# A 256-token stack on one core: the hybrid layers' activations, compression and pooling put in another order

## Chip, core and metric

The kernel runs on one core of a Trainium2 chip. The metric is device time in microseconds (us), the median of several executions. Inside the core five engines run side by side, each with its own queue of instructions: TensorE (PE, matrix products), VectorE (DVE), ScalarE (ACT), GpSimd (POOL) and SyncE (SP, which issues the DMAs). SBUF is the on-chip memory that all use; PSUM is the small memory that PE writes its products to.

## What is computed

A block of two layers (differential attention with a context, neighbourhood attention, each with a convolutional feed-forward part), then two hybrid layers. Sequence 256, width 1024, float32. The change touches the end of the block and the hybrid layers:

```python
def hybrid_layer(x, norm_g, w_in, ...):
    h = rmsnorm_2(x, norm_g)
    proj = h @ w_in
    (nsa_q, nsa_kv, nsa_g, pool_in, conv_in, fox_qkv, fox_f, gate_in, merge_in) = jnp.split(proj, split_at, axis=-1)
    o_nsa = nsa_mixer(nsa_q, nsa_kv, nsa_g, cmp_pos, cmp_w1, cmp_b1, cmp_w2, cmp_b2)
    o_pool = pool_mixer(pool_in, pool_w, pool_scale)
    c_x, c_b, c_c = jnp.split(conv_in, 3, axis=-1)
    o_conv = conv_mixer(c_x, c_b, c_c, conv_w)
    o_fox = fox_mixer(f_q, f_k, f_v, fox_f, fox_f_bias)
    for i, o in enumerate((o_nsa, o_pool, o_conv, o_fox)):
        branch = (o * jax.nn.silu(gates[:, :, i])) @ w_branch[i]
        term = jax.nn.sigmoid(merge[:, :, i]) * branch
        acc = term if acc is None else acc + term
    return x + acc @ w_out

def nsa_compress(k, pos_emb, w1, b1, w2, b2):       # inside nsa_mixer, for keys and for values
    blocks = k[:, idx] + pos_emb
    flat = blocks.reshape(B, nc, NSA_CMP_LEN * hd)
    return jax.nn.silu(flat @ w1 + b1) @ w2 + b2
```

The block before ends with `x = rmsnorm(x, norm_out)`, and the hybrid layer begins with a second norm of that.

## The kernel before

Activations lie transposed: `xT` has the 1024 features as eight chunks of 128 partitions, with the 256 tokens along the free axis. A float32 product is made from three products of rounded halves: a number is split into hi and lo, and `mm3` issues hi by hi (L335), weight hi by activation lo (L338) and weight lo by activation hi (L339). A projection of 128 output features ("a chunk") is 8 k steps of 3 matmuls, 24 matmuls of 256 columns.

Weights come by DMA from SP's queue into `raw` (3 buffers). `split` makes their halves: ACT copies to `whi` (L311), then `wlo` is raw minus whi (L314), on DVE, or on POOL for every `pool_every`-th split. Of `whi` and `wlo` there are 4 buffers each. PSUM has the tiles `acc` (2 buffers), `S` (3) and `misc` (3).

The order of each engine's instructions is not written out: a scheduler simulates the program and puts on each engine's queue what it finds ready first. Where the code asks for program order (`keep_in_program_order`) it keeps that.

The first hybrid layer (H0) starts inside the last down projection of the block: eight chunks of 33 matmuls each. As each chunk's residual lands in `xT` (L638, on DVE), `first_res` squares it for one norm (`norm_add`, ACT L474, summed on POOL L476), multiplies it by `norm_out` (L1035, DVE), squares it again for the second norm, and `scale_z` makes the hybrid's activation: a scaling by `g2` on DVE (L1161, tile `nt`), a rounded copy on ACT (L364) and a subtraction on DVE (L365), into `hhi` for both halves in H0 and `hlo` in H1. The norm factor itself is applied behind the products, as the broadcast tile `nbc` (L525 on PE, L530 on ACT). H1 starts the same way inside H0's output projection.

`hybrid` then runs, in this order: chunk 0 (`kvT`, keys and values to compress), chunks 1 and 2 (`kA`, `kB`, with `rope2`), the compression, chunks 3 and 4 (`q`), the product with `wvs` (48 matmuls of 400 columns, L1058 to L1062), NSA's scores (L1261), softmax (`softmax4`; POOL scales by L1531, PE transposes by L1535), FoX from chunks 5 to 8, the convolution from chunks 9 to 14, the pooling from chunks 15 and 16, the gates and the merge. The compression copies `kvT` into `big` with a position term (four DVE instructions, L1464), multiplies in two halves by DMAed weights (L1478, 16 products each), sums (L1485), applies a SiLU (DVE L1488, ACT L1492, DVE L1493 and L1494, tile `cu`) and multiplies again (L1496, L1497). The pooling makes sums over windows by doubling shifts on POOL (L1370, L1371), scales (L1376, L1377) and multiplies by `pool_w` (PE, L1379). In H0 eight POOL instructions (L1406) multiply `xT` by the norm's factor before the output projection needs it.

Of the kernel before, what the change touches and what calls it, by code (L numbers as in the profile page):

```python
# [195 lines left out]
def _layout_second(a, i):  # L196
    t1, wvs, mg, wb, wo, w1, w2, pw = [], [], [], [], [], [], [], []
    for l in range(DEPTH):
# [6 lines left out]
        tw = np.concatenate([kc, vc, ks, kw, kw, ks, q, fq, fk, cv, po, ga], axis=1)  # L205
# [22 lines left out]
class K:  # L228
# [355 lines left out]
    def ffn(self, l, halves, h_hi, h_lo, sts, mid=None, pre=(), bc=None):  # L584
# [4 lines left out]
        with self.pool(f"ffn{l}") as fp:  # L589
# [58 lines left out]
            for s in range(2):  # L648
# [22 lines left out]
                for m in range(8):  # L671
                    ws = self.wload(i["down"][l, s, m], [768, 640])
# [480 lines left out]
    def new_z(self, l):  # L1153

        z = self.t(self.hpool, [P, KC, 512], ("hhi", "hlo")[l], F32R)
        self.z = z[:, :, 0:T], z[:, :, T:512]

    def scale_z(self, l, kc):
        z = self.t(self.nrm, [P, T], "nt", bufs=5)
        k = l * KC + kc  # L1160
        self.nc.vector.tensor_scalar(z, self.xT[:, kc, 0:T], self.V("g2")[:, k : k + 1], None, op0=ALU.mult)  # L1161
        self.hilo(self.z[0][:, kc, :], self.z[1][:, kc, :], z)

    def hybrid(self, l, st, ns_out):
# [11 lines left out]
        self.pool_every, self.nsplit = 2, 1  # L1176
# [16 lines left out]
        def chunk(c):  # L1193

# [8 lines left out]
            w = self.split(queue.pop(0), 1024)  # L1203
            ps = (self.acc if 3 <= c < 99 else self.acc5)((P, T))
            self.proj(ps, w, zhi, zlo, T)
            return ps

# [43 lines left out]
        for kind, ty in (("slc", 1), ("win", 2)):  # L1251
            pT[kind] = t(hp, [P, 2, 4, T], "pT", bufs=2)
            for b in range(2):
                nk = P * (b + 1)
                sp = []
                for j in range(2):
                    s_ = self.sb((P, 2, T))
# [437 lines left out]
```

## Time and profile before

| | before |
|---|---|
| runs, us | 1627.94, 1636.3, 1638.55 (median 1636.3) |
| profiled execution, us | 1635.94 |
| span of its trace, us | 1634.0 |
| mean granted PE clock | 0.987 of full |
| H0 begins, at about | 1109.5 us |
| H1 begins, between | 1369 and 1405 us |

The trace shows one execution. A timeline row gives the start, the length, the engine, line, operation, output and inputs, and in brackets the idle time before it and what ended it. A line of the waits table gives an engine's waiting line, what it waited for, the total, the count and the longest wait. Lines L1161 and later are those of the kernel before; in the changed kernel the same code stands some 20 to 30 lines further down.

### The profile page before, as it was taken

How to read it: one execution, taken by the hardware profiler on the slowest of the kernel's cores; microseconds unless marked ns; L12 is line 12 of the kernel's file. 1: busy time of each engine (PE TensorE's matmuls, PEld its weight loads, DVE VectorE, ACT ScalarE, POOL GpSimd, SP SyncE). 2: the span in 40 equal slices, each digit the busy share in tenths (PEclk: the TensorE clock that was granted, in tenths of full speed). 3: DMA queues.
4: the chain of work that ended last, by engine and by line, in shares of the span. 5: the costliest groups of instructions: out<-in, count | busy, mean ns of one | idle time of the engine just before them, and what ended most of it. 6: DMA issues, size and time to landing. Idle time of an engine off the chain costs nothing.

```text
span 1634.0 us, 26740 instructions
## 1 busy us (share of the span) xinstructions
PE 1568.7 (96%) x10390; PEld 1367.3 (84%) x10390; DVE 1114.2 (68%) x1937; ACT 770.5 (47%) x1386; POOL 556.1 (34%) x505
## 2 busy tenths in 40 slices
PE   8999999899999999999999898997999999999998
PEld 5777677798888888877777887997899998899998
DVE  4657677678999994443445897567567668657665
ACT  3535454454422443334555653653654444545443
POOL 1122331331100111242234654667464226453222
PEclk9999999999999999999999999999999999999999
DMA  8523233225567532242322465546325555324552
GB/s 309 201 78 130 106 153 117 96 99 194 174 225 258 195 135 78 86 143 113 117 78 88 181 212 180 186 154 226 124 90 198 191 197 218 130 91 168 193 190 96
DMA packets 49486, 252.98 MB, mean 155 GB/s; under 512 B 5073, under 2 KB 8145, under 8 KB 31569
## 3 DMA queue, kind: packets, MB, share of 16 engines
q1 hardware_dynamic: 49360, 251.28, 43.0%
q8 instruction: 82, 1.34, 0.3%
q14 instruction: 44, 0.35, 0.1%
HBM read 250.21 MB, written 1.05 MB: 154 GB/s over the span
## 4 chain that ended last, share of the span: by engine, by line
PE 80%; DVE 11%; POOL 3%; issue 3%; ACT 2%; DMA 1%; SPq 0%; DVEq 0%; POOLq 0%; ACTq 0%
PE acc L335 11%; PE acc L338 11%; PE acc L339 11%; PE S L338 9%; PE S L335 9%; PE S L339 8%; PE S L1084 3%; DVE wlo L314 2%; PE misc L1131 1%; PE misc L1024 1%; PE S L1058 1%; PE misc L383 1%; PE S L1061 1%; DVE junk L436 1%; PE S L1062 1%
## 5 line engine op out<-in xcount | busy, mean ns | idle before, releaser
L311 ACT ACTIVATE whi<-raw 128x1024 fp32r<-128x1024 f32 (+2 forms) x374 | 374.1, 1006 | 428.9 <-PE S L338 161.9
L314 DVE TENSOR_TENSOR wlo<-raw,whi 128x1024 fp32r<-128x1024 f32 (+2 forms) x292 | 359.7, 1233 | 171.2 <-ACT whi L311 170.5
L335 PE MATMUL acc<-hhi,whi 128*128 128x256 f32 (+1 forms) x824 | 271.9, 330 | 1.7 <-DVE u L618 1.4
L338 PE MATMUL acc<-hlo,whi 128*128 128x256 f32 (+1 forms) x824 | 270.4, 328 | 0.3 <-DVE hlo L545 0.3
L339 PE MATMUL acc<-hhi,wlo 128*128 128x256 f32 (+1 forms) x824 | 268.9, 327 | 1.4 <-DVE wlo L314 1.4
L314 POOL TENSOR_TENSOR wlo<-raw,whi 128x1024 fp32r<-128x1024 f32 (+2 forms) x82 | 194.6, 2375 | 215.8 <-ACT whi L311 215.7
L335 PE MATMUL S<-hhi,whi 128*128 128x256 f32 (+1 forms) x560 | 178.3, 319 | 5.3 <-ACT hhi L364 3.2
L339 PE MATMUL S<-hhi,wlo 128*128 128x256 f32 (+1 forms) x560 | 177.7, 318 | 2.8 <-DVE wlo L314 2.3
L338 PE MATMUL S<-hlo,whi 128*128 128x256 f32 (+1 forms) x560 | 178.7, 319 | 0.1
L335 PEld LDWEIGHTS acc<-hhi,whi 128*128 128x128 f32 x824 | 155.5, 189 | 25.0 <-issue 10.0
L338 PEld LDWEIGHTS acc<-hlo,whi 128*128 128x128 f32 x824 | 154.8, 188 | 17.3 <-issue 5.3
L339 PEld LDWEIGHTS acc<-hhi,wlo 128*128 128x128 f32 x824 | 155.4, 189 | 15.8 <-DVE wlo L314 1.6
L624 POOL TENSOR_TENSOR u<-u,u 128x256 f32<-128x256 f32 (+1 forms) x46 | 59.2, 1288 | 273.8 <-ACT u L623 261.5
L436 DVE SCALAR_TENSOR_TENSOR junk<-araw,cb 128x1024 bf16<-128x1024 f32 x112 | 148.8, 1329 | 4.6 <-ACT cb L424 4.3
L335 PEld LDWEIGHTS S<-hhi,whi 128*128 128x128 f32 x560 | 105.1, 188 | 14.4 <-ACT hhi L364 3.4
L339 PEld LDWEIGHTS S<-hhi,wlo 128*128 128x128 f32 x560 | 105.0, 188 | 11.7 <-DVE wlo L314 2.9
L338 PEld LDWEIGHTS S<-hlo,whi 128*128 128x128 f32 x560 | 105.2, 188 | 7.4 <-DVE hlo L365 0.3
L1433 POOL TENSOR_TENSOR macc<-macc,mm 128x256 f32<-128x256 f32 x48 | 50.1, 1043 | 168.0 <-DVE mm L1431 168.0
L338 PE MATMUL acc<-hhi,whi 128*128 128x256 f32 x288 | 82.2, 286 | 0.0
L339 PE MATMUL acc<-hlo,wlo 128*128 128x256 f32 x288 | 81.7, 284 | 0.0
L335 PE MATMUL acc<-hlo,whi 128*128 128x256 f32 x288 | 81.4, 283 | 0.0
L335 PE MATMUL S<-ghi,whi 128*128 128x256 f32 (+1 forms) x231 | 76.3, 333 | 4.9 <-DVE xT L638 4.8
(414 smaller groups left out, 3777.7 us busy)
## 6 DMA issues: line engine op xcount, KB each, us to landing
raw<-in_up SPq DMA_DIRECT2D x44, 1024.0 KB, 4.8
raw<-in_mg SPq DMA_DIRECT2D x32, 1024.0 KB, 5.1
araw<-in_adav SPq DMA_DIRECT2D x56, 512.0 KB, 4.3
raw<-in_t SPq DMA_DIRECT2D x24, 1024.0 KB, 4.8
raw<-in_down SPq DMA_DIRECT2D x32, 704.0 KB, 4.1
raw<-in_ada SPq DMA_DIRECT2D x16, 1024.0 KB, 4.9
raw<-in_aqk SPq DMA_DIRECT2D x8, 1024.0 KB, 5.6
raw<-in_bqk SPq DMA_DIRECT2D x8, 1024.0 KB, 4.8
```

Of the source, the lines that this page charges most:

```text
L311: nc.scalar.activation(hi[:, :n], raw, AF.Copy)
L314: eng.tensor_tensor(lo[:, :n], raw, hi[:, :n].bitcast(F32), op=ALU.subtract)
L335: first = nc.tensor.matmul(ps, wh, x[0], start=start, stop=False)
L338: nc.tensor.matmul(ps, wh, x[1], start=False, stop=False)
L339: nc.tensor.matmul(ps, wl, x[0], start=False, stop=stop)
L383: nc.tensor.matmul(ps[32 * j : 32 * j + 32, 0:256], self.cs[:, 4 * r + j, :], raw[:, 4 * r + j, :], start=(r == 0), stop=(r == 1), tile_po ...
L436: nc.vector.scalar_tensor_tensor(junk, self.araw, 1.0, self.acb[0][:, c, :], op0=ALU.mult, op1=ALU.mult, accum_out=self.ada[l][:, v, k, c ...
L624: nc.gpsimd.tensor_tensor(us[0], us[0], us[1], op=ALU.mult)
L1024: nc.tensor.matmul(o[64 * j : 64 * j + 64, :], v[:, t, (2 * h + j) * 64 : (2 * h + j) * 64 + 64], pT[:, j, t, :], start=(t == 0), stop=(t ...
L1058: first = nc.tensor.matmul(ps, x[0], w[0], start=start, stop=False)
L1084: self.nc.tensor.matmul(sps[j][:, :n], q[a][r, qs], k[b][r, ks], start=(e == 0), stop=(e == 2))
L1433: nc.gpsimd.tensor_tensor(acc, acc, m, op=ALU.add)
```

## The change

Seven edits:

1. `scale_z` drops the scaled tile `nt`: ACT scales while it rounds, and DVE makes lo from `xT`, the gain and hi in one instruction.
2. The multiplication by `norm_out` leaves `first_res`: `g2` is multiplied by it once, the second norm squares with a gain, and POOL multiplies `xT` itself later, before the factor it already applied there.
3. `pool_every` is 0 from the sixth chunk of the last down projection on and through the hybrids' start; it is 2 again from FoX's chunks to the gates.
4. `chunks_late`: chunks 0 to 2 first run k steps 0 to 5, then steps 6 and 7 of each.
5. The compression is cut in two, `compress_in` behind the `q` chunks and `compress_out` behind `vs`.
6. The score loops go over the chunk first and the half second.
7. The pooling's chunks come before the convolution's (the weights are laid out in that order), its last product after the convolution.

```diff
-        tw = np.concatenate([kc, vc, ks, kw, kw, ks, q, fq, fk, cv, po, ga], axis=1)
+        tw = np.concatenate([kc, vc, ks, kw, kw, ks, q, fq, fk, po, cv, ga], axis=1)
...
-    def norm_add(self, s, x):
+    def norm_add(self, s, x, gain=1.0):
 
         nc = self.nc
         if s["k"] == 0:
             s["acc"] = self.t(self.nrm, [P, T], "nacc" + s["tag"], bufs=1)
-            nc.scalar.activation(s["acc"], x, AF.Square)
+            nc.scalar.activation(s["acc"], x, AF.Square, scale=gain)
         else:
             sq = self.t(self.nrm, [P, T], "nsq", bufs=3)
-            nc.scalar.activation(sq, x, AF.Square)
+            nc.scalar.activation(sq, x, AF.Square, scale=gain)
...
                 for m in range(8):
+                    if l == 1 and s == 1 and m == 5:
+                        self.pool_every = 0
                     ws = self.wload(i["down"][l, s, m], [768, 640])
...
-    def proj(self, ps, w, hhi, hlo, n, n0=0):
-        for kc in range(KC):
+    def proj(self, ps, w, hhi, hlo, n, n0=0, kcs=range(KC)):
+        for kc in kcs:
...
     def first_res(self, m):
 
-        nc = self.nc
         x = self.xT[:, m, 0:T]
+        self.scale_z(0, m)
         self.norm_add(self.fst[0], x)
-        nc.vector.tensor_scalar(x, x, self.V("nout")[:, m : m + 1], None, op0=ALU.mult)
-        self.norm_add(self.fst[1], x)
-        self.scale_z(0, m)
+        self.norm_add(self.fst[1], x, self.V("nout")[:, m : m + 1])
...
+        if l == 0:
+            self.nc.vector.tensor_tensor(self.V("g2")[:, 0:KC], self.V("g2")[:, 0:KC], self.V("nout"), op=ALU.mult)
 
     def scale_z(self, l, kc):
-        z = self.t(self.nrm, [P, T], "nt", bufs=5)
+
+        nc = self.nc
         k = l * KC + kc
-        self.nc.vector.tensor_scalar(z, self.xT[:, kc, 0:T], self.V("g2")[:, k : k + 1], None, op0=ALU.mult)
-        self.hilo(self.z[0][:, kc, :], self.z[1][:, kc, :], z)
+        x, g = self.xT[:, kc, 0:T], self.V("g2")[:, k : k + 1]
+        hi, lo = self.z[0][:, kc, :], self.z[1][:, kc, :]
+        nc.scalar.activation(hi, x, AF.Copy, scale=g)
+        nc.vector.scalar_tensor_tensor(lo, x, g, hi.bitcast(F32), op0=ALU.mult, op1=ALU.subtract)
...
-        self.pool_every, self.nsplit = 2, 1
+        self.pool_every, self.nsplit = 0, 1
...
-        def chunk(c):
-
+        def weights(c):
...
+            return self.split(queue.pop(0), 1024)
+
+        def chunk(c):
+
+            w = weights(c)
+            ps = self.acc((P, T))
             self.proj(ps, w, zhi, zlo, T)
             return ps
+
+        def chunks_late(cs, late):
+
+            ws, pss = [], []
+            for c in cs:
+                ws.append(weights(c))
+                pss.append(self.acc5((P, T)))
+                self.proj(pss[-1], ws[-1], zhi, zlo, T, kcs=range(KC - late))
+            for w, ps in zip(ws, pss):
+                self.proj(ps, w, zhi, zlo, T, kcs=range(KC - late, KC))
+            return pss
...
-        nc.vector.tensor_tensor(kvT[:, 0:T], chunk(0), bc, op=ALU.mult)
-        kA = rope2(chunk(1), 1, "kA")
-        kB = rope2(chunk(2), 1, "kB")
-        kcT, vc = self.compress(l, hp, kvT, wcp)
+        pss = chunks_late(range(3), 2)
+        nc.vector.tensor_tensor(kvT[:, 0:T], pss[0], bc, op=ALU.mult)
+        kA = rope2(pss[1], 1, "kA")
+        kB = rope2(pss[2], 1, "kB")
         q = [rope2(chunk(3 + c), 0, f"q{c}") for c in range(2)]
+        part = self.compress_in(l, hp, kvT)
...
+        kcT, vc = self.compress_out(l, hp, part, wcp)
         gate = t(hp, [P, 2, 12], "gate")
...
+                sp = [self.sb((P, 2, T)) for _ in range(2)]
+                for c in range(2):
+                    for j in range(2):
+                        r = slice(64 * j, 64 * j + 64)
+                        kk = kA if (kind == "slc") == (j == 0) else kB
+                        nc.tensor.matmul(sp[j][:, c, :nk], q[c][r, b * P : b * P + P], kk[r, 0:nk], start=True, stop=True)
...
+        self.pool_every = 2
         fq, fk = [], []
...
+        pls = []
         icnt = C("icnt").rearrange("p (c t) -> p c t", c=2)
         for c in range(2):
             u = s1()
-            nc.vector.tensor_tensor(u, chunk(15 + c), bc, op=ALU.mult)
+            nc.vector.tensor_tensor(u, chunk(9 + c), bc, op=ALU.mult)
...
+        o_pool = []
+        for c, pl in enumerate(pls):
...
+                self.tc.keep_in_program_order(
+                    nc.gpsimd.tensor_scalar(x, x, V("nout")[:, kc : kc + 1], 0.0, op0=ALU.mult, op1=ALU.add)
+                )
                 self.tc.keep_in_program_order(nc.gpsimd.tensor_tensor(x, x, b1, op=ALU.mult))
...
-                self.norm_add(ns_out, x)
                 if l == 0:
                     self.scale_z(1, m)
-                elif self.stop != "h1":
+                self.norm_add(ns_out, x)
+                if l == 1 and self.stop != "h1":
                     self.final_chunk(m)
...
-    def compress(self, l, hp, kvT, wcp):
-
-        nc, t, V, C = self.nc, self.t, self.V, self.C
+    def compress_in(self, l, hp, kvT):
+
+        nc, t, V = self.nc, self.t, self.V
...
+        return part
+
+    def compress_out(self, l, hp, part, wcp):
+
+        nc, t, V, C = self.nc, self.t, self.V, self.C
```

How the queues change, at the three places that matter. First DVE, in the last down chunks before H0. Names: `xT` the residual, `nt` the scaled tile, `hhi` the activation, `wlo` a weight's low half, `S` and `acc` PSUM tiles. Before:

```order
L638 SCALAR_TENSOR_TENSOR xT_71<-S_10125,ada_7_77,xT_71 128x256
L1035 TENSOR_SCALAR xT_71<-xT_71,vec_72 128x256
L1161 TENSOR_SCALAR nt_10167<-xT_71,vec_72 128x256
L365 TENSOR_TENSOR hhi_9836<-nt_10167,hhi_9836 128x256
L638 SCALAR_TENSOR_TENSOR xT_71<-S_10181,ada_7_77,xT_71 128x256
L314 TENSOR_TENSOR wlo_10362<-raw_10329,whi_10361 128x1024
```

and in the changed kernel:

```order
L638 SCALAR_TENSOR_TENSOR xT_71<-S_10111,ada_7_77,xT_71 128x256
L314 TENSOR_TENSOR wlo_10214<-raw_10207,whi_10213 128x640
L1167 SCALAR_TENSOR_TENSOR hhi_9836<-xT_71,vec_72,hhi_9836 128x256
L314 TENSOR_TENSOR wlo_10309<-raw_10306,whi_10308 128x1024
L638 SCALAR_TENSOR_TENSOR xT_71<-S_10164,ada_7_77,xT_71 128x256
L314 TENSOR_TENSOR wlo_10332<-raw_10306,whi_10331 128x1024
```

L1035, L1161 and L365 have become the one L1167, and splits that were POOL's stand between.

Second PE, at the compression's first product in H0. Names: `acc` a chunk's sum, `pT` the compression's weights, `big` the copied keys and values, `misc` PSUM. Before, both halves stand together behind a whole q chunk and the next begins behind them:

```order
L335 MATMUL acc_10505<-hhi_9836,whi_10501 128x256
L338 MATMUL acc_10505<-hhi_9836,whi_10501 128x256
L339 MATMUL acc_10505<-hhi_9836,wlo_10502 128x256
L1478 MATMUL misc_10439<-pT_10440,big_10433 32x128 x16
L1478 MATMUL misc_10439<-pT_10441,big_10433 32x128 x16
L335 MATMUL acc_10542<-hhi_9836,whi_10538 128x256
```

and in the changed kernel, where the two L525 make the broadcasts that `kvT` needs:

```order
L525 MATMUL misc_10289<-cst_69,nr_1789_10286 128x128 x2
L525 MATMUL misc_10294<-cst_69,nrstd_10277 128x128 x2
L338 MATMUL acc_10414<-hhi_9836,whi_10410 128x256
L339 MATMUL acc_10414<-hhi_9836,wlo_10411 128x256
L335 MATMUL acc_10414<-hhi_9836,whi_10410 128x256
L338 MATMUL acc_10414<-hhi_9836,whi_10410 128x256
L339 MATMUL acc_10414<-hhi_9836,wlo_10411 128x256
L1502 MATMUL misc_10488<-pT_10489,big_10482 32x128 x16
L1058 MATMUL misc_10527<-whi_10531,hhi_9836 128x400
```

The first half has moved up to the end of the first q chunk, five matmuls behind the broadcasts; the second half (not shown) stands 33 matmuls later. In H1 of the changed kernel both halves stand together, 44 matmuls behind the broadcast.

Third PE, at the compression's second product in H0. Names: `cpart` the first product copied to SBUF, `cu` the SiLU's tile, `kA`, `kB`, `q` the scores' inputs. Before:

```order
L335 MATMUL acc_10542<-hhi_9836,whi_10538 128x256
L1485 MATMUL misc_10478<-cst_1791_10287,cpart_10476 128x32
L338 MATMUL acc_10542<-hhi_9836,whi_10538 128x256
L339 MATMUL acc_10542<-hhi_9836,wlo_10539 128x256
L1261 MATMUL S_10650<-kA_10390,q_1836_10530 128x128
L1261 MATMUL S_10654<-kB_10427,q_1836_10530 128x128
L1261 MATMUL S_10678<-kA_10390,q_1836_10530 128x256
L1496 MATMUL misc_10486<-cu_10480,wcp_10322 128x16
L1497 MATMUL misc_10486<-wcp_10322,cu_10480 16x64
L1058 MATMUL misc_10573<-whi_10577,hhi_9836 128x400
```

and in the changed kernel:

```order
L1062 MATMUL misc_10528<-whi_10569,hhi_9836 128x400
L1514 MATMUL misc_10600<-cst_1783_10264,cpart_10525 128x32
L1281 MATMUL S_10627<-kA_10398,q_1815_10439 128x128
L1281 MATMUL S_10628<-kB_10404,q_1815_10439 128x128
L1281 MATMUL S_10627<-kA_10398,q_1821_10476 128x128
L1281 MATMUL S_10628<-kB_10404,q_1821_10476 128x128
L1281 MATMUL S_10655<-kA_10398,q_1815_10439 128x256
L1281 MATMUL S_10655<-kA_10398,q_1821_10476 128x256
L335 MATMUL acc_10826<-hhi_9836,whi_10822 128x256
```

The sum (L1485, now L1514) has moved behind the whole `wvs` product, and the second product (L1496, now L1525) stands 28 matmuls and two more score products behind it. On POOL, the pooling chain now stands between NSA's last scaling and FoX's first, with three splits between its pieces, and the eight pairs of `xT` products between the gates and the merge.

## Rows read from the trace of the kernel before

**Rows 1.** The page's first part: busy time, share of span, instructions per engine.
```profile
PE 1568.7 (96%) x10390; PEld 1367.3 (84%) x10390; DVE 1114.2 (68%) x1937; ACT 770.5 (47%) x1386; POOL 556.1 (34%) x505
```

**Rows 2.** Waits of PE, 1060 to 1370 us (total, times, longest).
```profile
PE S L335 <- ACT hhi L364: 3.2, 1, 3.2
PE misc L1496 <- issue: 2.4, 1, 2.4
PE misc L1478 <- issue: 1.6, 1, 1.6
PE misc L1379 <- POOL s L1377: 1.3, 1, 1.3
PE misc L1478 <- DVE big L1464: 0.7, 1, 0.7
PE S L339 <- POOL wlo L314: 0.5, 1, 0.5
```

**Rows 3.** Timeline of PE in H1: the rows with a wait, in brackets.
```profile
1373.54 0.38 PE L335 MATMUL S<-hlo,whi 128*128 128x256 f32 x1 [1.30 <-ACT hlo L364]
...
1385.38 1.08 PE L1478 MATMUL misc<-pT,big 128*32 128x128 f32 x32 [1.15 <-issue]
1387.18 1.08 PE L1478 MATMUL misc<-pT,big 128*32 128x128 f32 x32 [0.72 <-DVE big L1464]
...
1394.76 0.37 PE L1496 MATMUL misc<-cu,wcp 128*128 128x16 f32 x2 [2.40 <-issue]
...
1474.97 0.70 PE L1379 MATMUL misc<-s,wcp 128*128 128x256 f32 x2 [1.32 <-POOL s L1377]
```

**Rows 4.** Timeline of PE at H0's start (start, length, instruction, idle before).
```profile
1112.71 0.28 PE L339 MATMUL S<-hhi,wlo 128*128 128x256 f32 x1
1112.83 0.28 PE L338 MATMUL acc<-hhi,whi 128*128 128x256 f32 x1
1116.35 0.47 PE L335 MATMUL S<-hhi,whi 128*128 128x256 f32 x1 [3.23 <-ACT hhi L364]
```

**Rows 5.** Windows: us, busy time of each engine, then granted PE clock, DMA.
```profile
1116.36:1119.82 3.46, 3.46 (x16) 3.46 (x17) 3.02 (x7) 1.87 (x4) 1.08 (x4) 0.52 1.02 416
...
1140.42:1143.75 3.33, 3.33 (x12) 3.29 (x11) 1.13 (x8) 0.00 (x0) 0.00 (x0) 0.50 0.89 292
...
1396.50:1399.80 3.30, 3.30 (x11) 3.25 (x11) 0.13 (x1) 0.98 (x1) 0.00 (x0) 0.50 0.69 281
```

**Rows 6.** Timeline of DVE at H0's start.
```profile
1113.53 2.31 DVE L1161 TENSOR_SCALAR nt<-xT,vec 128x256 f32<-128x256 f32 x1
...
1119.19 0.35 DVE L1161 TENSOR_SCALAR nt<-xT,vec 128x256 f32<-128x256 f32 x1
```

**Rows 7.** Timeline of POOL at the same place.
```profile
1113.30 2.39 POOL L314 TENSOR_TENSOR wlo<-raw,whi 128x1024 fp32r<-128x1024 f32 x1
```

**Rows 8.** Timeline of DVE at H0's compression.
```profile
1127.63 0.40 DVE L1224 TENSOR_TENSOR kvT<-S,nbc 128x256 f32<-128x256 f32 x1
1128.07 4.21 DVE L1464 TENSOR_TENSOR big<-kvT,vec 64x256 f32<-64x256 f32 x4
...
1138.03 1.78 DVE L1494 TENSOR_SCALAR cu<-cu 128x32 f32<-128x32 f32 x1
```

**Rows 9.** Timeline of POOL: pooling chain's first and last instruction, then L1406.
```profile
1207.39 0.61 POOL L1370 TENSOR_TENSOR pw<-s 128x255 f32<-128x255 f32 x1
...
1219.26 0.79 POOL L1377 TENSOR_TENSOR s<-s,s 128x256 f32<-128x256 f32 x1
...
1239.00 7.80 POOL L1406 TENSOR_TENSOR xT<-xT,nbc 128x256 f32<-128x256 f32 x8
```

**Rows 10.** The page's costliest groups: weight splits on DVE (total, mean ns).
```profile
L314 DVE TENSOR_TENSOR wlo<-raw,whi 128x1024 fp32r<-128x1024 f32 (+2 forms) x292 | 359.7, 1233 | 171.2 <-ACT whi L311 170.5
```

**Rows 11.** Timeline of DVE at the first gate chunks.
```profile
1215.65 0.94 DVE L1396 SCALAR_TENSOR_TENSOR s<-s,s 128x256 f32<-128x256 f32 x1
```

**Rows 12.** Timeline of ACT at H0's broadcasts.
```profile
1127.17 0.83 ACT L530 ACTIVATE nbc<-misc 128x256 f32<-128x256 f32 x2 [1.16 <-PE misc L525]
```

More of the change, by code (lines that the diff above doesn't have):

```diff
@@ L1254, in hybrid @@
                 nk = P * (b + 1)
-                sp = []
-                for j in range(2):
-                    s_ = self.sb((P, 2, T))
-                    r = slice(64 * j, 64 * j + 64)
-                    kk = kA if (kind == "slc") == (j == 0) else kB
-                    for c in range(2):
-                        nc.tensor.matmul(s_[:, c, :nk], q[c][r, b * P : b * P + P], kk[r, 0:nk], start=True, stop=True)
-                    d = s_[:, :, nk - P : nk]
+                sp = [self.sb((P, 2, T)) for _ in range(2)]
[4 more added lines that the diff above has]
+                        nc.tensor.matmul(sp[j][:, c, :nk], q[c][r, b * P : b * P + P], kk[r, 0:nk], start=True, stop=True)
+                for j in range(2):
+                    d = sp[j][:, :, nk - P : nk]
                     cm = C("causal").rearrange("p (o t) -> p o t", o=1).to_broadcast([P, 2, P])
                     nc.vector.tensor_tensor(d, d, cm, op=ALU.add)
-                    sp.append(s_)
                 self.softmax4(hp, sp, nk, b, pT[kind], gate[:, b, 4 * ty : 4 * ty + 4])
@@ L1303, in hybrid @@
             fm = (fm0, fm1)[b]
-            sp = []
-            for j in range(2):
-                s_ = self.sb((P, 2, T))
-                r = slice(64 * j, 64 * j + 64)
-                for c in range(2):
-                    nc.tensor.matmul(s_[:, c, :nk], fq[c][r, b * P : b * P + P], fk[c][r, 0:nk], start=True, stop=True)
-                for c in range(2):
-                    hd = 2 * j + c
-                    nc.vector.scalar_tensor_tensor(
-                        s_[:, c, :nk], s_[:, c, :nk], cq[:, b, hd : hd + 1], fm[:, hd, :nk], op0=ALU.add, op1=ALU.add
-                    )
-                sp.append(s_)
+            sp = [self.sb((P, 2, T)) for _ in range(2)]
+            for c in range(2):
+                for j in range(2):
+                    r = slice(64 * j, 64 * j + 64)
+                    nc.tensor.matmul(sp[j][:, c, :nk], fq[c][r, b * P : b * P + P], fk[c][r, 0:nk], start=True, stop=True)
+            for hd in range(4):
+                d = sp[hd // 2][:, hd % 2, :nk]
+                nc.vector.scalar_tensor_tensor(d, d, cq[:, b, hd : hd + 1], fm[:, hd, :nk], op0=ALU.add, op1=ALU.add)
             self.softmax4(hp, sp, nk, b, fT, None)
@@ L1377, in hybrid @@
             nc.gpsimd.tensor_tensor(pl, pl, u, op=ALU.subtract)
+            pls.append(pl)
+        o_conv = []
+        cwv = V("cw2").rearrange("p (l k c) -> p l k c", l=DEPTH, k=3)
+        cxs, cbs = [], []
+        for c in range(2):
+            o = s1()
+            nc.vector.tensor_tensor(o, chunk(11 + c), bc, op=ALU.mult)
+            cxs.append(o)
+        for c in range(2):
+            o = s1()
+            nc.vector.tensor_tensor(o, chunk(13 + c), bc, op=ALU.mult)
+            cbs.append(o)
+        for c in range(2):
+            nc.gpsimd.tensor_tensor(cxs[c], cxs[c], bc, op=ALU.mult)
+            nc.vector.tensor_tensor(cxs[c], chunk(15 + c), cxs[c], op=ALU.mult)
+            y = t(ho, [P, T], f"cy{c}")
+            nc.vector.tensor_scalar(y, cxs[c], cwv[:, l, 2, c : c + 1], None, op0=ALU.mult)
+            for k in (1, 0):
+                sh = 2 - k
+                nc.vector.scalar_tensor_tensor(
+                    y[:, sh:T], cxs[c][:, 0 : T - sh], cwv[:, l, k, c : c + 1], y[:, sh:T], op0=ALU.mult, op1=ALU.add
+                )
+            nc.gpsimd.tensor_tensor(y, y, cbs[c], op=ALU.mult)
+            o_conv.append(y)
+        o_pool = []
+        for c, pl in enumerate(pls):
             ps = self.misc((P, T))
@@ L1405, in hybrid @@
                 x = self.xT[:, kc, 0:T]
+                self.tc.keep_in_program_order(
+                    nc.gpsimd.tensor_scalar(x, x, V("nout")[:, kc : kc + 1], 0.0, op0=ALU.mult, op1=ALU.add)
+                )
                 self.tc.keep_in_program_order(nc.gpsimd.tensor_tensor(x, x, b1, op=ALU.mult))
```

26 lines of the change are left out of this document (removed).

## The prediction

> **What bounds the kernel now.** I read the page's engine line first: TensorE (PE) is busy for 96% of the span, VectorE (DVE) for 68%, ScalarE (ACT) for 47%, GpSimd (POOL) for 34% [rows 1]. So little can be won: only PE's pauses, and the stretches in which its clock is low. The table of waits then says where PE pauses in the stretch that the change touches. Around the first hybrid layer (H0) six waits add up to 9.7 us [rows 2], in the second (H1) five more to 6.9 us [rows 3]. A wait is not the whole loss. PE's timeline at the start of H0 shows matmuls 0.12 us apart, then a gap of 3.52 us from start to start [rows 4]: 3.40 us lost for a listed wait of 3.23, so each pause costs about 0.17 us more than its wait. And pauses have an aftermath: in three stretches of 3.3 to 3.5 us the granted clock is half of full (1.2 instead of 2.4 GHz) [rows 5]. Two follow the 2.4 us waits of L1496 and one follows the 3.2 us wait of L335; behind the 1.3 us wait in H1 no such stretch was found. Half the clock costs half of such a stretch.
>
> Why PE waits: at the start of H0 the activation scaling L1161 takes 2.31 us on DVE, where the same form takes 0.35 us later [rows 6]. It lies under a POOL split L314 of 2.39 us [rows 7], and ACT's hi copy (L364), then DVE's lo subtraction (L365) and PE queue behind it. L1496, the compression's second product, waits for L1494, 1.78 us for 128x32 elements on DVE [rows 8], again under a POOL split. L1379 waits for the pooling chain, which runs on POOL from 1207.39 to 1220 [rows 9].
>
> **The change part by part.**
>
> *Shorter chain, no POOL splits at the start.* Three serial steps (L1161 on DVE, L364, L365) become two: ACT scales and rounds (after L1166), DVE makes lo in one scalar_tensor_tensor (L1167); eight times a layer. The eight L1035 leave DVE. The splits of the last three down chunks and of the hybrid's start all go to DVE: 13 POOL splits over both layers become DVE splits of up to 1.23 us each [rows 10], 16 us more DVE work. Does DVE keep up? A down chunk is 33 matmuls at 0.12, so 3.9 us of PE. DVE's share of a chunk is now 1408 columns of split (1408/1024 of 1.23 = 1.7), the residual L638 (0.5; L1224, which also reads 128x256 from PSUM, took 0.40 [rows 8]), and L1167, which the trace does not have: 0.35 at least (the free L1161 [rows 6]), 2.31 at most (the blocked one), and I take 0.94, that of the scalar_tensor_tensor L1396 with two inputs in SBUF [rows 11]. That is 3.1 us, 0.8 below PE's. At 2.31 it would be 4.5, over by 0.6 a chunk; but the POOL split that made 2.31 is gone, and what stays there are norm sums. The work is hidden by PE's matmuls; without that cover the 13 splits would cost up to 16 us. Late chunks: chunks 0 to 2 run their first six k steps, 54 matmuls (6.4 us), before any needs the last two activation chunks, so one late activation no longer stops PE. I count as gone in H0: 0.5 (L339) and 3.2 (L335); in H1: 1.3 (L335).
>
> The Trainium skill ("SBUF — State Buffer", section "Who interferes with whom") says that a DVE instruction with two SBUF inputs contends with a GpSimd one that reads SBUF, and that the loser waits for the whole instruction; this speaks against the new L1167, which has two. The trace agrees in size: L1396 took 0.94 beside POOL work. By the rule a norm sum of POOL can still block it; the sum stands at the 3.1 us above either way.
>
> *Compression in two parts.* Before, L1485, two of q1's matmuls and three score products stand between the first product and L1496; afterwards 39 matmuls of 400 columns stand between L1502's second half and L1514, and 28 more matmuls before L1525. At 0.15 us each (eleven of that kind took 3.30 us at half clock [rows 5], so half of 0.30) the 39 are 5.9 us, the 28 at 0.12 are 3.3: cover for chains of 2.4. Both 2.4 us waits go. The slow stretches behind them go too, and that behind the 3.2 us wait.
>
> *The first product moves, and its wait stays.* L1502 needs broadcast (nbc), kvT and four L1488. In H0 the broadcast L525 stands after 19 of q0's matmuls and L1502 five matmuls later. From L525 the chain is nbc 0.42 (half of 0.83 [rows 12]), kvT 0.40, two of four L1488 (the four took 4.21, so 1.05 each; 0.41 each if POOL is quiet, as L1224's 0.40) and about 0.6 of handoffs (three at 0.2): 2.2 to 3.5, less 0.6 of cover: 1.6 to 2.9. I take 2.45; before it was 1.6 + 0.7 [rows 2]. The second half has 33 matmuls of cover. In H1 both halves stand after q1 with 44 matmuls (5.2 us) of cover against 0.42 + 0.40 + 4.2 + 0.6 plus about 2 us of splits and shuffles ahead on DVE: 2.6 (0.4 to 3.0), before 1.1 + 0.7 [rows 3].
>
> *Pooling chunks first.* The chain of 12.6 us [rows 9] now starts six chunks earlier and its product (L1400) stands after FoX's output. The 1.3 us wait goes in both layers. But POOL now has chain, conv products, three splits of 2.4 and the FoX softmax scalings in some 18 us of PE: it ends about level with the transposes that need it. I also find NSA's softmax chain about 1.4 us closer to its transposes. I give back 0.7 us a layer, between 0 and 2.
>
> *Nothing:* 8 more POOL multiplies by nout (L1428), about 1 us each by L1406 [rows 9], lie ahead of the merge sums at 1239 while x is not read before the output projection, a whole stage later; if that cover were gone they would cost 8 us. Norm squares with a gain are the same ACT instruction. The interleaved scores: the four that differ already ran in pairs.
>
> **Sum.** Waits removed 7.4 (H0: 0.5 + 3.2 + 2.4 + 1.3) and 5.0 (H1: 1.3 + 2.4 + 1.3), refill 7 x 0.17 = 1.2, half of the slow stretches 3.46 + 3.33 + 3.30 = 5.0: 18.6 us. Given back: first product 0.15 in H0 and 0.8 in H1, a slow stretch behind H0's 2.45 us (1.65; as long a pause as L1496's 2.4, which had one both times), POOL 1.4: 4.0. Net 14.6 us. The profiled execution took 1635.94 us, its span 1634.0, beside a median of 1636.3, so no correction: **1621 us**.
>
> **The rivals.**
>
> *The pauses all go.* No slow stretch follows the first product (H0's own 1.6 + 0.7 had none), POOL is in time: 18.6 - 1.0 = 17.6, and up to 4.7 more if L1488 on a quiet POOL lets the first product come in time. 1614 to 1619. For it: POOL has no splits there any more. Against: the broadcast stands only five matmuls ahead. Chance 0.25.
>
> *The pauses move.* The same chains with less slack pause elsewhere: both first products near 3.0 with a slow stretch each (+2.6), FoX or NSA transposes late by 2 a layer (+2.6), one more slow stretch (1.65): 14.6 - 6.9, about 8 us left, 1628 (1626 to 1632). For it: the scheduler puts every consumer as close as its producers allow. Chance 0.23.
>
> *Slower: POOL becomes the bound between NSA and FoX.* Pooling chain, products, splits and scalings (22 us) stand on one queue within 18 to 20 us of PE, and the FoX transposes wait behind it. It decides when that queue runs half as long again, 11 us more: in both layers 22 us, with a slow stretch each 25, so 10 us slower, 1646. For it: contention stretched L1161 from 0.35 to 2.31 [rows 6] and may stretch POOL's work too. Against: only every second split is on POOL there, and the chain keeps its length of 12.6 us if it meets the same neighbours as before. Chance 0.09, and most of it ends below the 22 us, near 1636 to 1646.
>
> *It doesn't do what it says:* score interleaving is such a part; it counts for nothing already.
>
> **How the numbers follow.** The forecast holds 0.43 (own range 1617 to 1626). Less than 1% is about what a measurement here can't tell from no change: faster means below 1620. The first rival's 0.25 and a third of the forecast's (0.15) are faster: 0.40. Slower (above 1652) is the end of the last rival: 0.05. Within 1%: 0.55. The range 1612 to 1632 takes in the forecast and both middle cases, and leaves out most of the slower one.
>
> **What would show it.** At H0's start the 3.2 us and 0.5 us waits of L335 and L339 are gone, and no half-clock stretch at the start; L1525 and L1400 do not wait; L1502 waits 2.0 to 2.9 in H0 and about 2.6 in H1. Wrong it is if L1167 takes 2 us, if DVE splits stop PE in the last down chunks (waits for wlo L314), or if L1564 waits for L1560 by more than 2 us.

## The result, and the profile after

The changed kernel took 1616.0 us (median, 1613.8 to 1621.6), beside 1634.9 us for the kernel before: a ratio of 0.9877, 95% interval 0.9854 to 0.9901. That is 1.2% or about 19 us faster, where the forecast was 1621. The profiled execution's span fell from 1634.0 to 1614.7 us, by 19.3. All of that lies behind the start of the block's last down projection, whose first matmul stands at nearly the same time in both, here before and after:

```profile
1078.59 0.28 PE L335 MATMUL S<-ghi,whi 128*128 128x256 f32 x1
1078.81 0.28 PE L335 MATMUL S<-ghi,whi 128*128 128x256 f32 x1
```

From it to the end of the span are 555.4 us before and 535.9 us after, 19.5 less.

The page's first part, as [rows 1] (busy time, share of the span, instructions):

```profile
PE 1563.8 (97%) x10390; PEld 1364.8 (85%) x10390; DVE 1096.7 (68%) x1927; ACT 771.0 (48%) x1386; POOL 527.9 (33%) x500
```

PE has as many instructions as before and 4.9 us less busy time. The three half-clock stretches of [rows 5] are gone, about 5 us; but ahead of the hybrid layers, where the two kernels do the same, this execution has 6.8 us more at half clock than the one before, so the busy time of the whole span (at a mean granted clock of 0.988 beside 0.987) doesn't measure the change. The larger part of the 19.3 us is time in which PE no longer stands. The waits of PE from the end of the last down projection on, in the changed kernel, as [rows 2, 3] (total, times, longest):

```profile
PE misc L1502 <- issue: 2.3, 1, 2.3
PE acc L335 <- DVE kA L1236: 1.1, 1, 1.1
PE S L1329 <- ACT big L1553: 0.7, 2, 0.3
PE misc L1502 <- DVE big L1488: 0.4, 1, 0.4
```

Eleven waits of 16.6 us have become five of 4.5. The 3.2, 1.3 and 0.5 us waits at the starts, both 2.4 us waits of the compression's second product (now L1525) and both 1.3 us waits for the pooling are gone. What is left of size is the compression's first product. PE's timeline there, H0's row and then H1's two:

```profile
1125.42 1.08 PE L1502 MATMUL misc<-pT,big 128*32 128x128 f32 x32 [2.26 <-issue]
...
1371.98 0.35 PE L335 MATMUL acc<-hlo,whi 128*128 128x256 f32 x1 [1.13 <-DVE kA L1236]
...
1376.50 1.08 PE L1502 MATMUL misc<-pT,big 128*32 128x128 f32 x32 [0.45 <-DVE big L1488]
```

The 1.13 us is a new kind of wait: the second q chunk needs an `acc` buffer that `kA`'s chunk still holds, since the first three chunks now end together. And no half-clock stretch followed the 2.26 us. Windows of the changed kernel around that wait (us, busy time and count of PE, PEld, DVE, ACT, POOL, then PE's granted clock):

```profile
1122.00:1125.40 3.40, 1.16 (x11) 0.96 (x10) 3.13 (x7) 0.77 (x2) 2.71 (x4) 1.00 0.55 190
1125.42:1129.00 3.58, 3.58 (x48) 3.38 (x49) 3.52 (x6) 0.88 (x1) 3.01 (x4) 1.00 0.54 195
```

The new DVE step, grouped by line in the changed kernel (count, total busy, mean ns), H0 and H1, as [rows 6]:

```profile
L1167 DVE SCALAR_TENSOR_TENSOR hhi<-xT,vec,hhi 128x256 fp32r<-128x256 f32 x8 | 7.2, 910 | 0.0
L1167 DVE SCALAR_TENSOR_TENSOR hlo<-xT,vec,hlo 128x256 fp32r<-128x256 f32 x8 | 6.3, 798 | 0.0
```

The means are 0.91 and 0.80 us. Single ones take from 0.47 (POOL idle when it starts) over 0.96 (behind the start of a norm sum on POOL) to 1.79, this one beside a POOL split in a down chunk that still has one:

```profile
1092.47 1.79 DVE L1167 SCALAR_TENSOR_TENSOR hhi<-xT,vec,hhi 128x256 fp32r<-128x256 f32 x1
1091.80 2.18 POOL L314 TENSOR_TENSOR wlo<-raw,whi 128x640 fp32r<-128x640 f32 x1
```

So the 0.94 of [rows 11] was a fair mean, and nearly 2 us does occur where a POOL split is left.

### The profile page after: what moved, and what is told of

Same layout as the page of the kernel before. It is cut to its first block, busy times and chain, and to the rows that moved or that the text cites. A ratio compares the mean times of both kernels' runs of the same rounds, so it can differ in the third digit from the quotient of the medians.

```text
span 1614.7 us, 26688 instructions
## 1 busy us (share of the span) xinstructions
PE 1563.8 (97%) x10390; PEld 1364.8 (85%) x10390; DVE 1096.7 (68%) x1927; ACT 771.0 (48%) x1386; POOL 527.9 (33%) x500
## 4 chain that ended last, share of the span: by engine, by line
PE 86%; DVE 8%; issue 2%; ACT 2%; POOL 1%; DMA 1%; SPq 0%; DVEq 0%; POOLq 0%; ACTq 0%
PE acc L335 12%; PE acc L338 12%; PE acc L339 12%; PE S L338 9%; PE S L339 9%; PE S L335 9%; PE S L1084 3%; DVE wlo L314 2%; PE misc L383 1%; PE misc L1131 1%; PE misc L1026 1%; PE S L1058 1%; PE S L1061 1%; DVE junk L436 1%; PE S L1062 1%
## 5 line engine op out<-in xcount | busy, mean ns | idle before, releaser
L314 DVE TENSOR_TENSOR wlo<-raw,whi 128x1024 fp32r<-128x1024 f32 (+3 forms) x305 | 373.3, 1225 | 164.8 <-ACT whi L311 164.3
L314 POOL TENSOR_TENSOR wlo<-raw,whi 128x1024 fp32r<-128x1024 f32 (+1 forms) x69 | 166.5, 2414 | 193.1 <-ACT whi L311 187.8
```

The costliest lines, as they stand in the source:

```text
L314: eng.tensor_tensor(lo[:, :n], raw, hi[:, :n].bitcast(F32), op=ALU.subtract)
```

## The experiments

The times are medians; the ratio is to the kernel before, measured beside it. "Undone" means: the changed kernel with this edit put back. The last column is of the profiled execution alone: from the first matmul of the last down projection (the rows above) to the end. PE's instructions ahead of that matmul are the same in all these kernels, yet it starts anywhere between 1075.3 and 1083.8 us, so the last column compares two single profiles better than the spans do.

| kernel | us | ratio, 95% interval | span profiled | from the last down projection |
|---|---|---|---|---|
| kernel before | 1634.9 | 1 | 1634.0 | 555.4 |
| changed kernel | 1616.0 | 0.9877, 0.9854 to 0.9901 | 1614.7 | 535.9 |
| chain undone | 1620.5 | 0.9902, 0.9872 to 0.9933 | 1618.3 | 537.5 |
| no-POOL-splits undone | 1624.6 | 0.9922, 0.9895 to 0.9950 | 1620.6 | 539.4 |
| late chunks undone | 1617.0 | 0.9865, 0.9831 to 0.9899 | 1612.2 | 535.6 |
| compression undone | 1637.1 | 1.0018, 0.9997 to 1.0038 | 1635.0 | 556.9 |
| pooling order undone | 1614.5 | 0.9862, 0.9832 to 0.9892 | 1610.0 | 531.0 |
| the same, one more execution | 1618.8 | none | 1616.8 | 540.5 |
| compression and pooling order undone | 1626.3 | 0.9939, 0.9920 to 0.9958 | 1613.7 | 537.3 |
| before, no POOL splits alone | 1627.8 | 0.9929, 0.9905 to 0.9954 | 1622.6 | 544.3 |
| before, compression in two parts alone | 1627.1 | 0.9950, 0.9932 to 0.9968 | 1630.5 | 546.7 |
| first product behind wvs | 1611.5 | 0.9840, 0.9806 to 0.9874 | 1609.7 | 531.9 |
| the same again | 1612.2 | 0.9889, 0.9863 to 0.9916 | 1608.7 | 531.9 |
| the same, pooling order undone | 1614.4 | 0.9872, 0.9847 to 0.9898 | 1610.1 | 534.8 |

The order of the score loops (edit 6) was not undone by itself, and neither the shorter chain nor the late chunks were tried alone on the kernel before.

**The activation chain put back.**

```diff
-        nc.scalar.activation(hi, x, AF.Copy, scale=g)
-        nc.vector.scalar_tensor_tensor(lo, x, g, hi.bitcast(F32), op0=ALU.mult, op1=ALU.subtract)
+        self.nc.vector.tensor_scalar(z, self.xT[:, kc, 0:T], self.V("g2")[:, k : k + 1], None, op0=ALU.mult)
+        self.hilo(self.z[0][:, kc, :], self.z[1][:, kc, :], z)
```

(with norm_out back on DVE in `first_res`)

> The changed kernel with the activation chain of before put back: three steps (scaling on DVE, rounding on ACT, subtraction on DVE), and the multiplication by norm_out on DVE in the last down chunks; the splits stay on DVE, the last chunks stay late. Theory of the forecast (what made the 3.2 us and 1.3 us waits was the POOL split that held DVE, so that without it the long chain is quick, and late chunks cover the rest): 0 to 2 us slower than the changed kernel's 1616, no wait of a whole 2 us at the start of either hybrid layer. Rival (the three serial steps themselves are too long for the last down chunk): both waits come back, 3.4 + 1.5 us and a half-clock stretch of 1.7 us, 6 us slower, 1622.

It took 4 us more by the medians. The new row in its waits of PE:

```profile
PE misc L505 <- DVE naccx L476: 1.0, 1, 1.0
```

The 3.2 and 1.3 us waits do not come back. What comes is 1.0 us for the last norm sum, behind a longer DVE queue. The two intervals overlap, and from the last down projection on the profiled execution is only 1.6 us longer (537.5 beside 535.9), of which 1.0 stands in that wait: the chain is worth 1 to 4 us here, and the runs don't settle it closer. The rival, 6 us with both waits, is out by the trace.

**POOL splits put back.**

```diff
-                    if l == 1 and s == 1 and m == 5:
-                        self.pool_every = 0
...
-        self.pool_every, self.nsplit = 0, 1
+        self.pool_every, self.nsplit = 2, 1
```

> The changed kernel with every second split of the last down chunks and of the hybrids' start back on POOL. Contention theory: DVE's lo subtraction and the copies of the compression stand under POOL splits of 2.4 us again, waits of 1 to 2 us at several places of both layers, 3 to 8 us slower, 1619 to 1624. Rival (the two-step chain and the late chunks alone are enough, the place of the splits is free): within 2 us of 1616, no new wait above 0.7 us at the start.

It took 8.5 us more by the medians, 7 by the ratios; its profiled execution, the fastest of five, took 3.5 more from the last down projection on. Its waits of PE, and DVE at H0's compression:

```profile
PE misc L1500 <- issue: 5.1, 2, 2.8
...
PE S L339 <- POOL wlo L314: 0.2, 1, 0.2
```

```profile
1122.80 2.57 DVE L314 TENSOR_TENSOR wlo<-raw,whi 128x800 fp32r<-128x800 f32 x1
1125.29 0.41 DVE L1242 TENSOR_TENSOR kvT<-S,nbc 128x256 f32<-128x256 f32 x1
1125.74 4.52 DVE L1486 TENSOR_TENSOR big<-kvT,vec 64x256 f32<-64x256 f32 x4
```

A DVE split stands 2.57 us under a POOL split, where two of the kind take 1.88 together in the changed kernel, and `kvT` is late behind it. The first product waits 2.4 us in H0 and 2.8 in H1. The place of the splits matters in the finished kernel, but for the compression; at the starts 0.2 us is all that shows, so there the shorter chain and the late chunks are enough without it.

**Late chunks put back in order.**

```diff
-        pss = chunks_late(range(3), 2)
+        pss = chunks_late(range(3), 0)
```

> The changed kernel with chunks 0 to 2 running all eight k steps in order, nothing late. Theory that late chunks do the work at the start: the first chunks need the last activation after 24 to 48 matmuls, waits of 0.5 to 2 us for ACT or DVE at the start of each layer, 2 to 4 us slower than 1616, with a half-clock stretch if a wait passes 2.4 us. Rival (the scheduler interleaves the chunks anyhow, and the two-step chain is quick enough): within 1 us of 1616.

The same time: the rival. Its waits of PE in full:

```profile
PE misc L1502 <- issue: 2.2, 1, 2.2
PE S L1329 <- ACT big L1553: 0.7, 2, 0.3
```

With the chunks in order no start waits, and H1's 1.13 us for an `acc` buffer is gone too. In this execution a half-clock stretch does follow the first product:

```profile
1124.50:1127.90 3.40, 3.40 (x18) 2.53 (x17) 3.34 (x6) 0.00 (x0) 3.04 (x3) 0.53 0.08 29
```

Late chunks buy nothing that shows here: the two kernels differ by 1.0 us in the median, and undoing them takes H1's 1.13 us wait away.

**The compression whole again, in its old place.**

```diff
+        part = self.compress_in(l, hp, kvT)
+        kcT, vc = self.compress_out(l, hp, part, wcp)
         q = [rope2(chunk(3 + c), 0, f"q{c}") for c in range(2)]
-        part = self.compress_in(l, hp, kvT)
...
-        kcT, vc = self.compress_out(l, hp, part, wcp)
```

> The changed kernel with the compression whole again, between chunks 2 and 3 in the code as before. Forecast's theory: the second product waits 2.4 us in both layers and each wait draws a half-clock stretch: 2 x (2.4 + 0.17 + 1.66) = 8.5 us slower, 1624.5. Rival on the clock (the half-clock stretches of before needed the other pauses ahead of them, and come no more): 2 x 2.57 = 5.1 us slower, 1621. Rival (the waits came from POOL splits on which DVE's part of the chain was blocked, and those are gone): waits of 1 to 1.5 us, 2 to 3 us slower, 1619.

It lost 21 us, the whole gain and more than any theory said, and not where they said: the second product does not wait at all. Its waits of PE:

```profile
PE misc L1564 <- POOL big L1560: 7.4, 3, 3.8
PE S L1281 <- DVE q L1234: 3.1, 3, 1.4
PE misc L1502 <- issue: 2.3, 1, 2.3
PE acc L335 <- DVE kA L1236: 1.4, 2, 1.1
PE S L1281 <- ACT big L1553: 1.3, 1, 1.3
```

NSA's first scores now stand before `wvs`, and the pooling chain begins 10 us later than in the changed kernel. Its first sum there, and then here:

```profile
1169.37 0.61 POOL L1362 TENSOR_TENSOR pw<-s 128x255 f32<-128x255 f32 x1 [4.25 <-DVE s L1353]
1179.45 0.61 POOL L1362 TENSOR_TENSOR pw<-s 128x255 f32<-128x255 f32 x1 [9.46 <-DVE s L1353]
```

FoX has hardly moved (its first scaling L1560 starts at 1188.57, in the changed kernel at 1189.52), so it is the chain that has come onto FoX, and the scalings stand on POOL between the chain's second half (L1362, L1363) and splits:

```profile
1188.57 1.40 POOL L1560 TENSOR_SCALAR big<-big,nm 128x128 f32<-128x128 f32 x4
1189.94 0.60 POOL L1362 TENSOR_TENSOR pw<-pw 128x254 f32<-128x254 f32 x1
1190.49 0.18 POOL L1363 COPY pw<-pw 128x2 f32<-128x2 f32 x1
1190.63 2.33 POOL L314 TENSOR_TENSOR wlo<-raw,whi 128x1024 fp32r<-128x1024 f32 x1
```

Behind the pauses the clock falls; two of its five half-clock stretches, four of which last 6.8 us:

```profile
1133.50:1140.30 6.80, 6.80 (x22) 5.97 (x21) 3.27 (x15) 4.61 (x14) 0.00 (x0) 0.51 0.44 154
...
1191.60:1198.40 6.80, 4.23 (x21) 4.24 (x22) 0.00 (x0) 0.00 (x0) 6.64 (x12) 0.51 0.00 1
```

This is the prediction's slower rival, POOL as the bound between NSA and FoX, in a kernel where the forecast did not look for it. What share of the 21 us the waits have, and what share the stretches, is not taken apart.

**Compression and pooling order both undone.** The diff above and the next one together.

> The changed kernel with two edits undone: the compression whole and early, and the convolution before the pooling. With the compression alone undone it took 1637: the FoX transposes waited 7.4 us for POOL's scalings, which stood between pieces of the pooling chain, and five half-clock stretches lay behind the pauses. Theory (the two edits depend on each other: the early compression brings FoX forward, onto the pooling chain): without the chain there the 7.4 us and at least the two half-clock stretches behind them (6.8 us each, half of them lost) go, 1.3 us for each layer's pooling product come back: about 12 us faster than 1637, 1623 to 1627. Rival (the scores in front of the wvs product cost it by themselves): 1633 or more.

1626.3: the theory's number, and the waits for L1560 are gone from its list, while the pooling product waits instead. (That it was FoX that the early compression brought forward does not hold, as the rows above show: the chain came later.)

```profile
PE S L1281 <- DVE q L1234: 3.1, 3, 1.4
PE misc L1502 <- issue: 2.3, 1, 2.3
PE misc L1400 <- POOL s L1393: 2.2, 2, 1.3
```

The execution that was profiled took 1615.6 us, the other nine 1624.6 to 1631.9. It spaced its matmuls closer in the gates and merge, which is told under the next experiment:

```profile
1220.00:1320.00 100.00, 100.00 (x885) 100.00 (x884) 71.70 (x109) 50.12 (x76) 35.86 (x39) 1.00 0.57 201
```

So the two edits depend on each other: by the medians pooling first costs 11 us with the compression early, and about nothing with it late.

**The convolution before the pooling again.**

```diff
-        tw = np.concatenate([kc, vc, ks, kw, kw, ks, q, fq, fk, po, cv, ga], axis=1)
+        tw = np.concatenate([kc, vc, ks, kw, kw, ks, q, fq, fk, cv, po, ga], axis=1)
...
-            nc.vector.tensor_tensor(u, chunk(9 + c), bc, op=ALU.mult)
+            nc.vector.tensor_tensor(u, chunk(15 + c), bc, op=ALU.mult)
```

(and the pooling's block behind the convolution's)

> The changed kernel with the convolution's chunks before the pooling's again. Forecast's theory: the 1.3 us wait for the pooling chain comes back in both layers, 2 x 1.49 = 3.0 us slower, and POOL's crowding before FoX (two waits of 0.33 us) goes: 2.3 us slower, 1618. Rival (the crowding of POOL costs more than the wait that went): the same time or faster than 1616.

> The kernel with the convolution first once more, unchanged, one look. If the matmuls' distance in gates and merge is set by the program, it is 0.1133 us there again in both layers, and the span 1610; if it is chance which of the two distances an execution falls into, 0.1178 in one or both, and a span of up to 1620.

The two waits came back as the theory said, and FoX's 0.33 us went:

```profile
PE misc L1400 <- POOL s L1393: 2.6, 2, 1.3
```

Yet the median is not slower, and the profiled span is 4.7 us shorter. The same kernel profiled again, on another chip, had 1616.8 instead of 1610.0 us. Windows in the gates and merge of both layers, first execution and then the second, at full clock in both:

```profile
1220.00:1320.00 100.00, 100.00 (x884) 100.00 (x884) 70.77 (x107) 50.16 (x77) 36.13 (x40) 1.00 0.57 201
1480.00:1560.00 80.00, 80.00 (x708) 80.00 (x708) 55.70 (x83) 39.31 (x60) 17.70 (x17) 1.00 0.53 187
```

```profile
1220.00:1320.00 100.00, 100.00 (x852) 100.00 (x851) 69.06 (x103) 48.18 (x74) 35.43 (x38) 1.00 0.54 187
1480.00:1560.00 80.00, 80.00 (x682) 80.00 (x681) 53.69 (x80) 38.29 (x58) 17.07 (x18) 1.00 0.52 184
```

884 matmuls against 852 in 100 us: 0.1131 and 0.1174 us each, in one and the same program, with PE without a pause. Over the 1081 or so of a layer's gates and merge that is 4.7 us. The output projection behind them goes the other way: 181 matmuls in 21 us of the first execution (from 1334 us), 188 of the second (from 1338), which takes nearly 1 us of it back. So the closer spacing is worth about 4 us a layer, and it hides the 2.6 us of waits.

From the last down projection on the two executions took 531.0 and 540.5 us. Of these 9.5 us a half-clock stretch behind the second one's first product is 1.7, and the spacing the other 8. At equal spacing the order can be priced: the second execution without that stretch is 2.9 us longer than the changed kernel's 535.9, and the pair with the first product behind `wvs` (below) differs by 2.9 too (534.8 beside 531.9). Three single profiles thus say that pooling first is worth about 3 us, near the theory's 2.3; the medians cannot show it.

**One edit alone on the kernel before: no POOL splits.**

```diff
+                    if l == 1 and s == 1 and m == 5:
+                        self.pool_every = 0
...
-        self.pool_every, self.nsplit = 2, 1
+        self.pool_every, self.nsplit = 0, 1
```

> The kernel before with one edit alone: no POOL splits from the sixth chunk of the last down projection to FoX's chunks. Contention theory: the 0.5, 3.2 and 1.3 us waits at the starts go (5.5 us with their refills) with the first half-clock stretch (1.7), and the chain before the second product is no longer blocked (the 1.78 us instruction becomes short), so that those waits fall from 2.4 to about 1 (2.8) and lose their half-clock stretches (3.3): 13 us faster than before, 1622. Rival (the chain's own length): less than 4 us faster, 1631 or more.

About 11 us faster (11.1 from the last down projection on), near the contention theory's 13 and far from the rival. The 3.2 us wait is down to 1.2, H1's 1.3 is gone, and the 128x32 instruction before the second product, 1.78 us in [rows 8], is short:

```profile
1134.35 0.17 DVE L1497 TENSOR_SCALAR cu<-cu 128x32 f32<-128x32 f32 x1
```

The second product no longer waits, but the scores that now stand just ahead of it do, for q, 1.8 us in H0 and 2.2 in H1:

```profile
PE S L1263 <- DVE q L1217: 4.2, 3, 2.2
```

So the theory's number is partly luck. Its half-clock stretches did not go: 3.4 us follow H0's wait for q, and 10.2 and 3.4 us stand in H1, where the hybrid layers of before had three of 3.4. All waits of PE fell from 16.6 to 10.9 us, which is about half of the 11; where the rest comes from was not found.

**One edit alone: the compression in two parts.** The diff of the change for `compress_in` and `compress_out`, on the kernel before. It is not quite one edit: the score loops of edit 6 are in it, and a few instructions keep the changed kernel's place in the code (the copy of `kvT` behind all three first chunks, the pooling's last products behind both its chains).

> The kernel before with one edit alone: the compression in two parts, the first behind the q chunks, the second behind vs (and the loops of the scores). Forecast's theory: both 2.4 us waits of the second product go with their refills and the two half-clock stretches behind them, 8.5 us faster than before; the first product still waits. Rival (with the splits on POOL the copies of kvT are held up as before, and the first product's wait, now in front of less cover, takes what was won): less than 4 us faster.

8 us faster by the ratio, and 8.7 from the last down projection on, as the forecast's 8.5. The two half-clock stretches behind L1496's waits are gone too; the one at H0's start stays. Its waits of PE are nearly those of before without L1496's:

```profile
PE S L335 <- ACT hhi L364: 3.2, 1, 3.2
PE misc L1494 <- issue: 2.8, 2, 1.6
PE misc L1395 <- POOL s L1388: 2.6, 2, 1.3
PE S L335 <- ACT hlo L364: 1.3, 1, 1.3
```

**The first product one step later.**

```diff
-        part = self.compress_in(l, hp, kvT)
...
+        part = self.compress_in(l, hp, kvT)
         vs = t(ho, [P, 2, 400], "vs")
```

> The changed kernel with the first part of the compression one step later in the code, behind the wvs product. The waits left in the changed kernel are 2.3 us (first product, H0) and 1.1 + 0.4 us (H1). Theory: they are waits of a consumer put too near, and go: 2.3 + 1.6 + refills 0.5 = 4.4 us faster, 1612. Rival (what is behind is late instead: the compressed keys reach NSA's scores too late, or the kA wait of 1.1 us is one for a PSUM buffer and stays): 2 us faster or none.

> The kernel with the first part of the compression behind the wvs product, once more with more rounds, beside the kernel before. If the 4.4 us of waits that it removes are real, the ratio to before is 0.984 again, with an interval that lies below the changed kernel's 0.9877 (about 1611 beside 1616). If it was the luck of which executions had the matmul distance of 0.1133 us, the ratio is 0.987 to 0.989.

> The first part of the compression behind the wvs product (1611.5 us when done alone on the changed kernel) and the convolution before the pooling. By waits: the two FoX score waits of 0.33 us go and two waits of 1.3 us for the pooling product come: 1614. Rival, from the trace of the kernel with the convolution first, where the matmuls' distance was 0.1133 instead of 0.1178 us through gates and merge of both layers, from the 1.3 us wait on: the same happens here, 2 x 1080 matmuls x 0.0045 = 9.7 us less, 1604.

Its waits of PE, first kernel:

```profile
PE S L1281 <- ACT big L1553: 1.2, 2, 0.8
PE S L1329 <- ACT big L1553: 0.7, 2, 0.3
```

The first product's 2.3 us and H1's 1.1 and 0.4 are gone; 1.2 us for the scores is new. The medians are 1611.5 and 1612.2, some 4 us below the changed kernel's 1616.0, and both profiled executions took 531.9 us from the last down projection on, 4.0 less than the changed kernel's 535.9, where the theory said 4.4. Luck with the spacing is out: in all three the matmuls of the gates and merge stand 0.118 us apart. The ratios are 0.9840 and 0.9889, around the changed kernel's 0.9877, since the kernel before itself lay between 1630.6 and 1638.6 in these comparisons. The two kernels did not run beside each other, so the gain over the changed kernel is shown by the traces and not settled by the ratios. With the pooling order undone as well it took 1614.4, the number by waits; the rival's closer spacing did not come (852 matmuls in the 100 us from 1220).

## Why the prediction was right, point by point

**The bound and the direction** were right: PE's pauses and half-clock stretches were what could be won, and nearly all of the listed ones went.

**The starts (3.2, 1.3, 0.5 us)** went as forecast. That POOL splits made them is shown on the kernel before: with the splits alone moved, 3.2 fell to 1.2 us and the other two went. But in the finished kernel they are removed twice: with the splits back on POOL only 0.2 us of them returns, and with the long chain back none. The working credited the late chunks with a share, and none shows; undoing the chain costs 1.6 us by the traces and 4 by the medians (the intervals overlap).

**The compression's second product** went, and alone it measured 8 us against 8.5. The working missed that two edits remove the same wait: without POOL splits the product doesn't wait either, though PE then pauses just ahead of it for q. Added up, the gains measured one at a time (11 and 8) leave nothing for the other edits. The working's 0.15 us for a matmul of 400 columns was too short (48 of them start within 8.6 us in H1, 0.18 apart), which only lengthens the cover it counted on.

**The first product** was 2.45 us in H0 by the sum and measured 2.26. H1's 2.6 was mis-sized (its own terms add up to 2.4): it measured 1.13 + 0.45, the first part of which is a wait for a PSUM buffer that the working did not see.

**The half-clock stretch behind it** (1.65 us) was the step that failed. It did not come in this execution, nor in the profiles with the chain, the POOL splits or the compression undone; it came with the late chunks undone, with compression and pooling order undone, and in one of two executions with the pooling order undone, after waits of 2.2 and 2.3 us. A wait of 2.8 us in H1, with the POOL splits undone, had none either. It should have stood in the sum as a chance, about one in three, not as a certainty drawn from two cases.

**POOL before FoX** was given 1.4 us, and no wait for POOL's scalings shows in the changed kernel. The 0.7 us that stands there is two waits of FoX's scores (L1329) for ACT's exponentials (L1553). They go when the pooling order is undone, so they are a price of that order, but not by the queue that the working named. The rival "slower, POOL becomes the bound" was avoided here: with the compression early the same queue cost 7.4 us of waits.

**The new DVE step** at 0.94 measured 0.91 and 0.80 in the mean, with 1.79 once beside a POOL split, and DVE kept up with the down chunks: no wait for `wlo` shows there. The x multiplications on POOL and the norm gain show in no wait.

With the half-clock stretch left out and the measured sizes put in, the sum is 18.6 + 0.3 - 0.7 = 18.2 us (H1's first product was 0.3 shorter than before, FoX's scores cost 0.7), against 19.3 between the two spans. About 1 us is unexplained. So the case that came is the first rival, "the pauses all go" (1614 to 1619), though its reason was half right: no half-clock stretch followed and POOL was in time, but the first product still waited. In another execution the stretch can come, and 1.7 us of the gain goes with it.

## What to carry to other kernels

When one engine is the bound, list its waits, and ask of each whether another engine's long instruction holds the one that it waits for; undoing that move cost more here than undoing the shorter chain (3.5 against 1.6 us by the traces, 8.5 against 4.5 by the medians). Compare single profiles from the same instruction on, not by their spans. Edits that remove waits are not additive: two may remove the same wait, and one may be harmless only because of another, so undo each from the finished kernel as well as adding it alone to the old one. Move a consumer back by what its producers really take, not to the first place that a schedule allows.

## What the runs showed of the hardware that I had not expected

The distance of back-to-back 128x256 matmuls has two values at full clock, about 0.113 and 0.118 us. One value holds over stretches of 100 us, and two executions of one program differed in it, in the windows above. In the gates and merge the lower value stands in two of the fourteen profiled executions, the first of these two and the one with compression and pooling order undone; in both it began right behind the wait for the pooling product, in both layers. In five others the same wait stands and the value stayed. The chip alone does not set it, since the two came from two chips that also gave the higher value. Behind gates and merge at the lower value the output projection of H0 ran at the higher one; in ten of the other twelve executions it was the other way round. What sets it was not found. It is worth about 4 us a layer, which is as much as several of the edits, and a difference of that size between two single profiles is no evidence on an edit.

A pause of 2.2 to 2.4 us for the first product in H0 was followed by a half-clock stretch in three of eight profiled executions of the changed kernel and its variants.
